# Attention scores of the first token tile ahead of the second tile's last queries

## The chip, the core and the metric

One core of one Trainium2 chip runs the whole program in one launch. The metric is device time in microseconds, median of the runs shown. TensorE (PE) multiplies; its weight loads are listed as PEld. VectorE is DVE, ScalarE is ACT, GpSimd is POOL, and SyncE (SP) issues most transfers.

## What is computed

The reference is an encoder trunk of two layers on 256 tokens of width 1024, in float32: per layer a SwiGLU feed-forward (width 2816), a mixer, and another SwiGLU, each followed by a layer norm of `alpha*x + y`. The mixer of layer 0 is a bidirectional mLSTM; that of layer 1, the stage that is changed, is windowed attention with 16 query heads, 4 key heads, a linear distance bias and a sink logit per head:

```python
p = x @ w_in                                    # queries 1024, keys 256, values 256
s = einsum(q, k) * HEAD_DIM ** -0.5 - slopes * dist
s = where(valid, s, MASK_VALUE)                 # |t - s| <= 128
m = maximum(max(s), sink)
pe = exp(s - m)
attn = pe / (sum(pe) + exp(sink - m))
return einsum(attn, v) @ w_out
```

## The kernel before

**Arithmetic.** Every float32 operand of a large product is split into a high and a low part (`w_hi`, `w_lo`; ACT copies the high part, DVE subtracts for the low one), and `mm3` (line 626) makes three products of it. Tokens lie in two tiles of 128 (`t`), and `xT` holds x transposed. Weights come in words of 128 x 1024; `Weights.split` (line 406) splits a word into a ring of ten buffers.

**Stages.** Six: feed-forward, mLSTM, feed-forward, feed-forward, attention (stage 4, `attn`, line 1223), feed-forward. The end of a stage's second tile (`pending`) is called inside the next stage's first products.

**The attention.** `proj(t, m)` (line 1260) is a projection of 512 columns for token tile t, 24 products into one bank of PSUM: m = 0 makes keys and values, m = 1 the first eight heads' queries, which DVE scales on the way out into `qd`, a tile with the tag `sc`. `k_turn(t)` and `q_turn(t)` (1281, 1287) transpose keys and queries of tile t, four transposes each, into `kk` and `q2`, high part by ACT, low part by DVE. `q_rest` (1295) makes the last eight heads' queries, transposed already, as products of 256 columns; the argument says which part of its 32 pieces, three products each, is made. `scores(j, between)` (1318) makes the scores of step j, heads 2j and 2j+1, for both token tiles: for each tile six products on 64 of the 128 rows (one head in each half of the rows: high x high, high x low, low x high), POOL copies the sink beside them, and DVE adds the bias and takes the row minimum, one instruction a head. Then ACT takes the exponentials, four instructions, with their sums in `sm`. Each score product reads the keys of all 256 tokens, so both `k_turn`s come before it.

Then, step after step (line 1406), `scale` (POOL) divides by the sums, `turn` transposes the weights, `values` multiplies by v and `out_proj` multiplies by the output weights. `fill` puts pieces of `q_rest` and `out_proj` between. The sequence ahead of that loop is

```python
proj(1, 0); k_turn(0); q_turn(0); proj(1, 1)
k_turn(1); q_rest(range(QC[0])); q_turn(1)      # QC[0] is 5
```

**What sets the order.** None of these calls issues anything. `Program` records every operation, and `issue` (line 307) issues them in the order of `ORDER`, a list of steps whose running sums are the numbers of the recorded operations: 6658 of them, for all stages. Each engine works through its own in that order. `SLOTS` says which buffer each tile takes: banks of PSUM (`p`, eight), weights' words, the ring, the attention's `sc` (six), `nm` and `sm` (three).

Of the kernel before, what the change touches and what calls it, by code (L numbers as in the profile page):

```python
# [9 lines left out]
F32 = mybir.dt.float32  # L10
FR = mybir.dt.float32r
AF = mybir.ActivationFunctionType
OP = mybir.AluOpType
# [18 lines left out]
SW = 1  # L32
CT = [0, 1]
# [230 lines left out]
        "503250679835"),  # L264
    "t.0": ("00413152105244534524043241352"),
    "stats": ("000101110010"),
    "mv": ("011101100000"),
    "rs": ("110011110010"),
    "raw.1": ("03101030130120310231230123103210"),
    "wt.1": ("0132"),  # L270
# [1208 lines left out]
```

## Time and profile before

| | us |
|---|---|
| median of 3 runs | 918.23 (917.81 to 919.16) |
| the profiled execution | 918.0 |
| its span, first to last instruction | 916.3 |

The attention's projections begin at about 650 us of the span, its scores run from 670 to 711 us, and the last feed-forward's products are under way at 740 us. The profile's rows give start, duration, engine, operation, and the tile written from the tiles read; nearly all rows carry line 316, the one in `issue` that issues recorded operations, so one goes by tiles: `kk_hir` and `kk_lor` are the keys' parts, `q2r` the queries, `p` a bank of PSUM, `sc` the scores and, under the same tag, keys and queries before they are transposed (products written `p<-ident,sc` are transposes). Records of products overlap, since they are pipelined: what counts is how far apart they start.

### The profile page before, as it was taken

Reading aid. Unit: us, or ns where it says so; the run is one execution under the profiler, and the core shown is the slowest. Engines: PE = TensorE matmul, PEld = TensorE weight load, DVE = VectorE, ACT = ScalarE, POOL = GpSimd, SP = SyncE. Lnnn points to the kernel's source line nnn. Section 1 sums busy time; section 2 is a strip of 40 time slices with the busy share of each in tenths; the row PEclk is TensorE's granted clock in tenths of the full one; section 3 lists DMA queues with packets and bytes.
Section 4 is the critical chain, followed back from the end, with each engine's and each line's share of the span. In section 5 each row is a group of like instructions: output and inputs, shape, how many; then the busy total and the mean of one; then the engine's idle time right before and its main releaser. Section 6 shows DMA issues by size and latency. Waiting matters only on the chain.

```text
span 916.3 us, 12374 instructions
## 1 busy us (share of the span) xinstructions
PE 906.1 (99%) x4397; PEld 750.8 (82%) x4397; DVE 813.9 (89%) x989; ACT 576.9 (63%) x796; POOL 144.2 (16%) x191
## 2 busy tenths in 40 slices
PE   9999999999999999999999999999999999999996
PEld 7888888889988888888888888888887788888885
DVE  7999899987788999889999989899898899987996
ACT  6767567547664577566647674774588657665570
POOL 0211211110101111111011111110345211201110
PEclk9999999999999999999999999999999999999999
DMA  9999798657346899979788998997552287998951
GB/s 336 326 276 293 220 294 209 215 168 259 96 163 241 237 240 230 307 222 277 222 275 207 276 268 249 264 231 247 170 200 70 70 266 204 270 284 236 300 140 46
DMA packets 100654, 208.51 MB, mean 228 GB/s; under 512 B 6864, under 2 KB 21216, under 8 KB 100592
## 3 DMA queue, kind: packets, MB, share of 16 engines
q1 hardware_dynamic: 82816, 173.82, 54.3%
q0 software_dynamic: 17632, 33.64, 22.1%
q8 instruction: 34, 0.56, 0.2%
q10 hardware_dynamic: 144, 0.26, 0.1%
q14 instruction: 28, 0.23, 0.1%
HBM read 206.65 MB, written 1.05 MB: 227 GB/s over the span
## 4 chain that ended last, share of the span: by engine, by line
PE 98%; DVE 1%; DMA 0%; issue 0%; ACT 0%; POOLq 0%; POOL 0%; DVEq 0%
PE p L316 98%; DMA s_raw<-in_at_w_out_dram 0%; DVE x L316 0%; DVE w_lo L316 0%; ACT w_hi L316 0%; POOLq L1475 0%; ACT q2r L316 0%; DVE stats L316 0%; DVE mv L316 0%; POOL ji L316 0%; DVE ident L316 0%; DVE rs L316 0%; POOLq L316 0%; DVEq L316 0%; POOLq L1466 0%
## 5 line engine op out<-in xcount | busy, mean ns | idle before, releaser
L316 ACT CAST w_hi<-s_raw 128x1024 fp32r<-128x1024 f32 x240 | 246.4, 1051 | 94.0 <-PE p L316 51.0
L316 DVE TENSOR_TENSOR w_lo<-s_raw,w_hi 128x1024 fp32r<-128x1024 f32 x240 | 287.3, 1221 | 14.4 <-PE p L316 6.9
L316 DVE TENSOR_TENSOR w_lo<-w_raw,w_hi 128x1024 fp32r<-128x1024 f32 (+1 forms) x166 | 198.5, 1207 | 24.8 <-ACT w_hi L316 19.9
L316 ACT CAST w_hi<-w_raw 128x1024 fp32r<-128x1024 f32 (+1 forms) x166 | 171.0, 1041 | 74.2 <-PE p L316 41.9
L316 PE MATMUL p<-w_hi,xT_hi 128*128 128x512 f32 x512 | 194.6, 395 | 0.0
L316 PE MATMUL p<-w_lo,xT_hi 128*128 128x512 f32 x512 | 194.4, 396 | 0.0
L316 PE MATMUL p<-w_hi,xT_lo 128*128 128x512 f32 x512 | 194.2, 394 | 0.0
L316 PE MATMUL p<-w_lo,h_hir 128*128 128x512 f32 (+1 forms) x323 | 119.8, 390 | 0.0
L316 PE MATMUL p<-w_hi,h_hir 128*128 128x512 f32 (+1 forms) x323 | 119.5, 390 | 0.0
L316 PE MATMUL p<-w_hi,h_lor 128*128 128x512 f32 (+1 forms) x323 | 119.4, 390 | 0.0
L316 PEld LDWEIGHTS p<-w_lo,xT_hi 128*128 128x128 f32 x512 | 96.1, 188 | 19.6 <-DVE w_lo L316 0.3
L316 PEld LDWEIGHTS p<-w_hi,xT_lo 128*128 128x128 f32 x512 | 96.1, 188 | 19.3 <-DVE xT_lo L316 0.3
L316 PEld LDWEIGHTS p<-w_hi,xT_hi 128*128 128x128 f32 x512 | 96.0, 188 | 19.3 <-ACT xT_hi L316 0.6
L316 POOL DMA_DIRECT2D s_raw<-in_ffn_w_in_dram x42 | 50.9, 1220 | 295.8 <-DVE w_lo L316 109.9
L316 PE MATMUL p<-w_hi,S_hir 128*128 128x512 f32 x256 | 96.2, 390 | 0.0
L316 PE MATMUL p<-w_hi,S_lor 128*128 128x512 f32 x256 | 96.1, 389 | 0.0
L316 PE MATMUL p<-w_lo,S_hir 128*128 128x512 f32 x256 | 95.1, 389 | 0.0
L316 PEld LDWEIGHTS p<-w_lo,h_hir 128*128 128x128 f32 x323 | 60.7, 188 | 12.2
L316 PEld LDWEIGHTS p<-w_hi,h_lor 128*128 128x128 f32 x323 | 60.7, 188 | 12.1
L316 PEld LDWEIGHTS p<-w_hi,h_hir 128*128 128x128 f32 x323 | 60.5, 188 | 12.2 <-ACT h_hir L316 0.2
L316 POOL DMA_DIRECT2D w_raw<-in_ffn_w_in_dram x22 | 27.3, 1260 | 192.5 <-DVE s_raw L316 104.3
L316 PEld LDWEIGHTS p<-w_hi,S_hir 128*128 128x128 f32 x256 | 48.1, 188 | 10.9 <-ACT t L316 1.0
(189 smaller groups left out, 1204.3 us busy)
## 6 DMA issues: line engine op xcount, KB each, us to landing
s_raw<-in_ffn_w_in_dram SPq DMA_DIRECT2D x97, 512.0 KB, 6.7
w_raw<-in_ffn_w_in_dram SPq DMA_DIRECT2D x62, 512.0 KB, 6.0
s_raw<-in_ffn_w_out_dram SPq DMA_DIRECT2D x61, 512.0 KB, 5.8
s_raw<-in_ffn_w_in_dram POOLq DMA_DIRECT2D x42, 512.0 KB, 7.3
w_raw<-in_ffn_w_out_dram SPq DMA_DIRECT2D x27, 512.0 KB, 5.4
w_raw<-in_ml_w_in_dram SPq DMA_DIRECT2D x24, 512.0 KB, 4.6
w_raw<-in_ffn_w_in_dram POOLq DMA_DIRECT2D x22, 512.0 KB, 7.2
s_raw<-in_ffn_w_in_dram SPq DMA_DIRECT2D x18, 256.0 KB, 5.1
```

Source lines behind the costliest of these rows:

```text
L316: f(*args, **kw)
```

## The change

`proj` may make a part of its products (`ks`) and hold its bank until the rest; `scores` is taken apart into `half(j, t, banks)`, the six products, POOL's copy and DVE's two instructions for one tile, and `expo(j, t)`, ACT's two; `early(j)` makes both for tile 0 in two banks of its own. With EARLY = 2, steps 0 and 1 have their first tile made early, and their place in the loop makes only the second one, in two more banks. `nm` and `sm` have four buffers.

```diff
-            def proj(t, m):
-                ps = wbank()
-                for k in range(8):
+            def proj(t, m, ks=range(8)):
+                ps = held.pop((t, m)) if ks[0] else wbank()
+                for k in ks:
...
-                if m == 0:
+                if ks[-1] < 7:
+                    held[t, m] = ps
+                elif m == 0:
...
+            def early(j):
+                half(j, 0, [wbank((128, 2, S))[:, 0] for _ in range(2)])
+                expo(j, 0)
+
             def scores(j, between):
...
+                if j < EARLY:
+                    half(j, 1, [wbank((128, 2, S))[:, 0] for _ in range(2)])
                 else:
-                    ps = [wbank((128, 2, S)), wbank((128, 2, S))]
...
+                    ps = [wbank((128, 2, S)) for _ in range(2)]
+                    for t in range(2):
+                        half(j, t, [p[:, t] for p in ps])
                 if between is not None:
                     between()
...
+                for t in range(1 if j < EARLY else 0, 2):
+                    expo(j, t)
...
-            proj(1, 1)
+            proj(1, 1, range(4))
             k_turn(1)
+            early(0)
+            proj(1, 1, range(4, 8))
+            for j in range(1, EARLY - 1):
+                early(j)
             q_rest(range(QC[0]))
+            if EARLY > 1:
+                early(EARLY - 1)
             q_turn(1)
```

`ORDER` and `SLOTS` are replaced whole, for all six stages; the number of operations stays 6658. Read through ORDER, TensorE's queue around the place is, with the number of products of each call (S(j,t) is the score block of step j and tile t):

| | TensorE's queue from the keys' second transposes on |
|---|---|
| before | k_turn(1) 4, proj(1,1) 3, q_rest 1, proj 1, q_rest 1, proj 3, q_rest 8, q_turn(1) 3, S(0,0) 6, q_turn(1) 1, q_rest 11, S(0,1) 6 with one of S(1,0), q_rest 16, S(1,0) 5, q_rest 10, S(1,1) 6 |
| after | k_turn(1) 4, proj(1,1) 1, q_rest 1, proj 12, S(0,0) 6, proj 7, q_rest 10, q_turn(1) 4, q_rest 10, S(1,0) and S(0,1) 12, q_rest 27, S(1,1) 6 |

Ahead of k_turn(1) the old queue has 17 of proj(1,1)'s 24 products and two products of q_rest, the new one 4 and none.

More of the change, by code (lines that the diff above doesn't have):

```diff
@@ L32 @@
 SW = 1
+EARLY = 2
 CT = [0, 1]
@@ L39 @@
 ORDER = (
[207 rows of a table removed]
[206 rows of a table added]
 )
 SLOTS = {
-    "raw.0": ("210375894160ab235798a3b1270586492706351792840a63b5824a0376b12a950371"),
-    "p": ("3275714003260343071152161261516216215555634170524061732573604751024052375104126373674045206243753410"
-        "2763544201141022414410422206137147250124731601566516506116051015601476432475321340245765271430621547"
-        "0166232663126613312621641232570623056410072302032720330732720"),
+    "raw.0": ("321074689152ab307468a3b2140768951804372860951a43b7805a1394b20a671392"),
@@ L253 @@
+    "p": ("7726143024501264721103513501305151053355147653637504627132156370460357046253741062615726304572156721"
+        "5436075712552157251117552517204352641253602217242741271471274744756274530135254730175670532470514605"
+        "16513744024002742207074247001546753460245732060210216062162106164"),
     "h_hir.0": ("01001"),
-    "h_lor.0": ("10101"),
-    "w_hi": ("6768095130964720852931483069218659270964306517289436702158934670215893407659821437580692134758061923"
-        "4785062193478506219837540621973810465279318042736519807562314982365017834296750186293475018629438127"
-        "0654873912605478392106547832051964785320164958370621450938614825793061482579306148290753684219705638"
-        "2479015632074986513207498653027148953046287150439620954268031942356795218036479531028647593820135792"
-        "713098467532"),
@@ L260 @@
-    "w_lo": ("2108424370857191438825409670813427259384713240631879043512685973014268597302749175403682415970821346"
-        "9518026734591082673495018764253941806592834192587316048197236415381087862513209874362150789430524617"
-        "9038274569308172540936807215678943256178024314690173457806213896510478912634805971698430569780416358"
-        "0217945620437986510243798601354276809481396725394082419852763017596803541729506814578192034578021309"
-        "503250679835"),
-    "t.0": ("00413152105244534524043241352"),
@@ L266 @@
[L266 to L270, printed above, removed]
-    "a_hir.1": ("1010"),
-    "a_lor.1": ("1010"),
-    "den.1": ("1101"),
-    "hst.1": ("1111"),
-    "hmv.1": ("0101"),
-    "hrs.1": ("1110"),
-    "h_hir.2": ("0101001010"),
-    "h_lor.2": ("1010110101"),
-    "raw.2": ("8975460317258a96043b86a594703192b47136540891b72a369827ba4035a716ba5803196b425986103b42a716073294a5b9"
-        "32845472a36918b0546198230b5a06743218"),
@@ L281 @@
-    "t.2": ("2301524103213320314352354203204125301153451204025545243544"),
-    "sc.4": ("4212152104531245301452"),
-    "raw.4": ("34203524421301520354"),
-    "nm.4": ("01001202"),
-    "sm.4": ("21212120"),
-    "pr0_hir.4": ("01111110"),
-    "pr0_lor.4": ("00111111"),
-    "pr1_hir.4": ("11101010"),
-    "pr1_lor.4": ("10001011"),
-    "o.4": ("01110101"),
-    "h_hir.5": ("10101"),
-    "h_lor.5": ("01001"),
-    "raw.5": ("102305321b48520639705367a0ab218a90b3871542ab90a68731a9506b059584726b"),
@@ L294 @@
-    "t.5": ("13505412501444130321035034514"),
+    "h_lor.0": ("01010"),
+    "w_hi": ("4874953029716840190254792863407284952713051684937205468193720546819372056413089275106438971205634879"
+        "1208469352174806935248170639452817064589231756804912685097483129865047329157604832915760483901574836"
+        "2091425783601924570863197428610359742681503948076251497306218457930621845793162085491384627503861942"
+        "7053681907425639817024563981720456389170245861937204517396238052317496058271843605927864130527986354"
+        "127834906178"),
@@ new lines @@
+    "w_lo": ("8236425073987610431028793481054310826875931208496351427806981532476091824596471308476529137048269351"
+        "0748690312478569301457826397510462873054218950732456827269241307265103472852910437856214093785042819"
+        "0327628054913267081459365209872314986150472983560791407836952478691325097814920356784193425670278145"
+        "9236071495286731045928763195280476359025417920638059786342701984652793174065928316270618453978269124"
+        "785904265197"),
+    "t.0": ("13015334223502455505412340234"),
@@ new lines @@
+    "stats": ("001011100111"),
+    "mv": ("111001101001"),
+    "rs": ("100010001111"),
+    "raw.1": ("13233213213210122330312103213021"),
+    "wt.1": ("1203"),
+    "a_hir.1": ("1010"),
+    "a_lor.1": ("0101"),
+    "den.1": ("0010"),
+    "hst.1": ("0110"),
+    "hmv.1": ("1110"),
+    "hrs.1": ("0001"),
+    "h_hir.2": ("1010111001"),
+    "h_lor.2": ("0101010101"),
+    "raw.2": ("859764031726859b0a34865b9a7130429a7016ba3842970516482597b01a8536b97a01364b9276a4310b9285341b0269875a"
+        "026794b0825a367195a14632079b0685120b"),
@@ new lines @@
+    "t.2": ("4430251042543542345220120340242312503145315235440352440533"),
+    "sc.4": ("0512432025134021354021"),
+    "raw.4": ("32013214312403150245"),
+    "nm.4": ("01201123"),
+    "sm.4": ("02003013"),
+    "pr0_hir.4": ("01100000"),
+    "pr0_lor.4": ("10011011"),
+    "pr1_hir.4": ("11100001"),
+    "pr1_lor.4": ("10100101"),
+    "o.4": ("01101011"),
+    "h_hir.5": ("01001"),
+    "h_lor.5": ("10101"),
+    "raw.5": ("210332150498b125732b631ba847502a9840a2385067ba4912786a94030bb31594a2"),
@@ L295 @@
+    "t.5": ("35123042540233523553024000125"),
 }
@@ L1258, in attn @@
             pieces = []
-            def proj(t, m):
-                ps = wbank()
-                for k in range(8):
+            held = {}
+            def proj(t, m, ks=range(8)):
+                ps = held.pop((t, m)) if ks[0] else wbank()
+                for k in ks:
                     if t == 0 and m == 1 and k == PEND[bound[0] - 1]:
@@ L1316, in flush @@
                 del lows[:n]
-            def scores(j, between):
-                g = j // 2
-                nm = tile_([128, 2, 2], F32, "nm", bufs=3)
-                sm = tile_([128, 2, 2], F32, "sm", bufs=3)
-                if SW:
-                    p1 = wbank((128, 2, S))
-                    ps = [wbank((128, 2, S)), p1]
-                else:
-                    ps = [wbank((128, 2, S)), wbank((128, 2, S))]
-                for t in range(2):
-                    for n_, (qe, ke) in enumerate(((0, 0), (0, 1), (1, 0))):
-                        for a in range(2):
-                            r = slice(64 * a, 64 * a + 64)
-                            nc.tensor.matmul(ps[a][:, t], q2[r, j, qe, tok(t)], kk[ke][r, g], start=n_ == 0, stop=n_ == 2)
-                    sc[j, t] = tile_([128, 2, 320], F32, "sc", bufs=6)
-                    nc.gpsimd.tensor_copy(sc[j, t][:, :, S], neg_sink[:, 2 * j:2 * j + 2])
-                    for a in range(2):
-                        h = 2 * j + a
-                        nc.vector.tensor_tensor_reduce(sc[j, t][:, a, 0:S], ps[a][:, t], dist[:, t], -slope[h], neg_sink[:, h:h + 1],
-                                                       OP.add, OP.min, accum_out=nm[:, t, a:a + 1])
@@ new lines, in attn, with half @@
+            sums_ = {}
+            def half(j, t, banks):
+                g = j // 2
+                if j not in sums_:
+                    sums_[j] = tile_([128, 2, 2], F32, "nm", bufs=4), tile_([128, 2, 2], F32, "sm", bufs=4)
+                nm, sm = sums_[j]
+                for n_, (qe, ke) in enumerate(((0, 0), (0, 1), (1, 0))):
+                    for a in range(2):
+                        r = slice(64 * a, 64 * a + 64)
+                        nc.tensor.matmul(banks[a], q2[r, j, qe, tok(t)], kk[ke][r, g], start=n_ == 0, stop=n_ == 2)
+                sc[j, t] = tile_([128, 2, 320], F32, "sc", bufs=6)
+                nc.gpsimd.tensor_copy(sc[j, t][:, :, S], neg_sink[:, 2 * j:2 * j + 2])
+                for a in range(2):
+                    h = 2 * j + a
+                    nc.vector.tensor_tensor_reduce(sc[j, t][:, a, 0:S], banks[a], dist[:, t], -slope[h], neg_sink[:, h:h + 1],
+                                                   OP.add, OP.min, accum_out=nm[:, t, a:a + 1])
@@ new lines, in expo @@
+            def expo(j, t):
+                nm, sm = sums_[j]
+                for a in range(2):
+                    nc.scalar.activation(sc[j, t][:, a, 0:S + 1], sc[j, t][:, a, 0:S + 1], AF.Exp, bias=nm[:, t, a:a + 1],
+                                         scale=-1.0, accum_out=sm[:, t, a:a + 1])
+                if t == 1:
+                    stat[j] = sm
+            def early(j):
+                half(j, 0, [wbank((128, 2, S))[:, 0] for _ in range(2)])
+                expo(j, 0)
+            def scores(j, between):
+                if j < EARLY:
+                    half(j, 1, [wbank((128, 2, S))[:, 0] for _ in range(2)])
+                else:
+                    ps = [wbank((128, 2, S)) for _ in range(2)]
+                    for t in range(2):
+                        half(j, t, [p[:, t] for p in ps])
@@ L1338, in scores @@
                 if between is not None:
                     between()
-                for t in range(2):
-                    for a in range(2):
-                        nc.scalar.activation(sc[j, t][:, a, 0:S + 1], sc[j, t][:, a, 0:S + 1], AF.Exp, bias=nm[:, t, a:a + 1],
-                                             scale=-1.0, accum_out=sm[:, t, a:a + 1])
-                stat[j] = sm
+                for t in range(1 if j < EARLY else 0, 2):
+                    expo(j, t)
             def scale(j):
```

413 rows, old and new, of the table ORDER are left out of this document.

## The prediction

> **What bounds the kernel now.** I read the page first, then TensorE's waits, then the stages of the attention by windows, then TensorE's timeline there, product by product. S(j,t) below is the score block of step j (two heads) for token tile t: six products on 64 rows of the array.
>
> ```profile
> span 916.3 us, 12374 instructions
> ...
> PE 906.1 (99%) x4397; PEld 750.8 (82%) x4397; DVE 813.9 (89%) x989; ACT 576.9 (63%) x796; POOL 144.2 (16%) x191
> ...
> PE 98%; DVE 1%; DMA 0%; issue 0%; ACT 0%; POOLq 0%; POOL 0%; DVEq 0%
> ```
> TensorE is busy for 906.1 of 916.3 us and is 98% of the chain that ended last. Its waits are all in two rows:
>
> ```profile
> PE p L316 <- DVE ident L316: 1.5, 1, 1.5
> PE p L316 <- DMA s_raw<-in_at_w_out_dram: 0.3, 1, 0.3
> ```
> The first is the start of the program. The second lies in the attention, and just where the change works. So there is almost no idle time to take away; what else can move is how closely products follow each other, which "busy" hides, since the records of pipelined products overlap. The plain spacing, in the attention's first projections:
>
> ```profile
> 650.25 0.39 PE L316 MATMUL p<-w_hi,xT_hi 128*128 128x512 f32 x1
> 650.48 0.39 PE L316 MATMUL p<-w_hi,xT_lo 128*128 128x512 f32 x1
> 650.71 0.39 PE L316 MATMUL p<-w_lo,xT_hi 128*128 128x512 f32 x1
> ```
> A product of 512 columns lasts 0.39 us and starts 0.23 us after the one before. The windows (columns: busy us and count of PE, PEld, DVE, ACT, POOL, then granted clock, DMA share, GB/s):
>
> ```profile
> 660.00:680.00 20.00, 19.70 (x139) 16.95 (x138) 18.62 (x34) 16.62 (x33) 3.96 (x10) 1.00 0.71 237
> 680.00:700.00 20.00, 20.00 (x133) 15.38 (x131) 17.73 (x48) 16.53 (x48) 10.33 (x24) 1.00 0.14 53
> 700.00:720.00 20.00, 20.00 (x113) 14.63 (x112) 17.91 (x46) 16.47 (x48) 13.35 (x25) 1.00 0.45 148
> ```
> PE is full throughout, DVE nearly: 18.62 of 20 us where the change puts its first scores. DVE is the engine that may be late if its order turns out badly.
>
> **The change part by part.** *Work.* The pieces that are moved are the same: S(0,0) and S(1,0), their four row minima on DVE, four exponentials on ACT, two small copies on POOL. No product, copy or transfer is added or dropped, so TensorE keeps its 4397 products. What changes is the order, and ORDER is replaced whole: all six stages are planned anew. Walking the running sums of both ORDERs through the recorded calls, I find the other stages shuffled only locally, on TensorE by at most 43 places. There the waits table shows nothing to gain; a loss is possible where a weight part comes late.
>
> *Visits.* TensorE goes to the 64-row score blocks and back. What one visit costs, S(1,1):
>
> ```profile
> 676.62 0.28 PE L316 MATMUL p<-xT_hi,w_hi 128*128 128x256 f32 x1
> 676.74 0.28 PE L316 MATMUL p<-xT_lo,w_hi 128*128 128x256 f32 x1
> 676.95 0.39 PE L316 MATMUL p<-kk_hir,q2r 64*128 64x256 f32 x2
> 677.17 0.28 PE L316 MATMUL p<-kk_lor,q2r 64*128 64x256 f32 x2
> 677.29 0.28 PE L316 MATMUL p<-kk_hir,q2r 64*128 64x256 f32 x2
> 677.50 0.51 PE L316 MATMUL p<-xT_hi,w_lo 128*128 128x256 f32 x2
> 677.84 0.28 PE L316 MATMUL p<-xT_hi,w_hi 128*128 128x256 f32 x1
> ```
> Ordinary products of 256 columns start 0.12 us apart (676.62 to 676.74), and score products run two abreast at the same step (677.17 to 677.29). From 676.74 to 677.84 pass 1.10 us, in which three ordinary products (0.36) and three pairs (0.36) would fit in 0.72. A visit costs 1.10 - 0.72 = 0.38 us beside its work. Counted from ORDER, the 16 blocks make 20 visits before: S(0,1) and S(1,0) are cut 7 + 5, S(5,0), S(5,1) and S(6,1) are cut in two, two and three. After, they make 18: S(1,0) and S(0,1) share one visit of twelve products, S(4,0), S(6,0) and S(6,1) are cut in two. Two visits less are 2 x 0.38 = 0.76 us gained, all of it on TensorE and so on the path. Within the visits, products of the same half that follow each other don't pair; counted in steps, 58 before and 54 after, at 0.12 at most 0.48 us more. I take nothing for it, as other transitions (a product behind transposes) shift too, and keep 0.5 us for the range, also on the other side.
>
> The Trainium skill, page "TensorEngine Tiling (Array Packing)", section "Key Properties", says that changing the tiling mode, not just the tile, drains the TensorE; the 0.38 us above agree. By that rule the change as it is called is bad: scores called tile 0 and tile 1 back to back, and now two steps' halves stand apart, two visits more, which would give 918.23 + 0.76 = 919.0. But the queue follows ORDER, not the calls.
>
> *The first visit.* It is dearer than the others:
>
> ```profile
> 669.30 0.55 PE L316 MATMUL p<-ident,sc 128*128 128x128 f32 x3
> 670.15 0.38 PE L316 MATMUL p<-kk_hir,q2r 64*128 64x256 f32 x2 [0.30 <-DMA s_raw<-in_at_w_out_dram]
> 670.34 0.31 PE L316 MATMUL p<-kk_lor,q2r 64*128 64x256 f32 x2
> ...
> 670.69 0.33 PE L316 MATMUL p<-ident,sc 128*128 128x128 f32 x1
> ```
> Three transposes of some 0.1 us would let the scores start at 669.6 or, with the 0.09 of a usual entry (676.95 - 676.74 - 0.12), at 669.7; they start at 670.15, 0.45 us late. The change doesn't take away what the first reader of the keys waits for, it puts that reader earlier. I cost it at no gain, with 0.45 us as the other end, and its worse turn among the rivals.
>
> *Where S(0,0) goes, and what must be ready.* Against the old queue, 7 projection products, 11 of the last queries' and 3 transposes move behind it: 7 x 0.23 + 11 x 0.12 + 3 x 0.1 = 3.2 us earlier. It reads the keys of both tiles. The old path from the keys' transposes:
>
> ```profile
> 666.04 0.60 PE L316 MATMUL p<-ident,sc 128*128 128x128 f32 x4
> ```
> ```profile
> 666.68 0.59 ACT L316 CAST kk_hir<-p 128x512 fp32r<-128x512 f32 x1 [0.60 <-PE p L316]
> ...
> 668.23 1.28 ACT L316 ACT_TABLE_LOAD   x1
> ```
> ```profile
> 663.69 2.36 DVE L316 TENSOR_TENSOR w_lo<-s_raw,w_hi 128x1024 fp32r<-128x1024 f32 x2 [0.19 <-ACT w_hi L316]
> 665.97 1.22 DVE L316 TENSOR_TENSOR w_lo<-w_raw,w_hi 128x1024 fp32r<-128x1024 f32 x1
> 667.10 0.41 DVE L316 TENSOR_TENSOR v0r<-p,v0r 128x256 fp32r<-128x256 f32 x1
> 667.44 0.68 DVE L316 TENSOR_TENSOR kk_lor<-p,kk_hir 128x512 fp32r<-128x512 f32 x1
> 668.55 0.69 DVE L316 TENSOR_TENSOR sc<-p,qs_row 128x512 f32<-128x512 f32 x1 [0.43 <-PE p L316]
> ```
> The low part of the keys is there at 668.12, 2.08 us after the transposes begin. In the new queue these four are followed by 13 projection products and one of the last queries', 0.4 + 13 x 0.23 + 0.12 = 3.5 us, then S(0,0): 1.4 us to spare. DVE has to keep up 3.2 us earlier for that; its new order puts two of the weight parts (1.22 each) behind the keys and v1's low part (0.41, that of v0 above) ahead, 2.0 us of the 3.2. Behind S(0,0) stand the second half of the projection, 7 x 0.23 = 1.6 us, and 10 products of the last queries, 1.2 us, ahead of the queries' transposes, which need the scaling at 668.55's kind (0.69): covered. The table load of 1.28 us stands in the new ORDER far ahead, among stage 3's last copies. It leaves the crowded stretch, but ACT is not on the path: nothing.
>
> The row minima and exponentials, per piece:
>
> ```profile
> L316 DVE CUSTOM_DVE_ANT_0 sc<-p,dist,neg_sink x32: 467/480/485, 670.8 to 711.9; 128x256 f32<-128x256 f32 x32
> L316 ACT ACTIVATE sc<-sc,nm x32: 495/506/522, 672.5 to 713.0; 128x257 f32<-128x257 f32 x32
> ...
> L316 POOL COPY sc<-neg_sink x16: 178/187/519, 666.7 to 710.9; 128x2 f32<-128x2 f32 x16
> ...
> L316 POOL TENSOR_TENSOR dist<-sc,sc x1: 2140/2140/2140, 651.1 to 651.1; 128x512 f32<-128x512 f32 x1
> ```
> Four minima at 0.48 and four exponentials at 0.51 come some 3 us sooner. One of S(0,0)'s two minima stands ahead of the queries' scaling on DVE (0.48 us of delay against 1.2 us of cover), the other behind it and behind one weight part; the exponentials on ACT stand behind the copy of tile 1's queries. The distances are ready at 651.1 + 2.1 = 653.3, long before. Nobody waits for the exponentials sooner than before: the first transposes of weights still come behind the queries' products. So the softmax gains a lead that TensorE, which has fill work, cannot turn into time. SP's transfers only change places among the attention's weights; DMA share is 0.71 there, not full.
>
> *Sum:* -0.76 (visits) + 0 (pairs, first visit, other stages). The profiled execution took 918.0 us, 1.7 outside its span; it becomes 917.2. The median of the runs is 918.23, 0.23 higher: **917.4 us**.
>
> **The rivals.** *No effect:* the saved visits are eaten by small shifts elsewhere. For it: the whole gain is 0.08% of the time, and five stages are replanned. It gives 918.2.
>
> *More:* pairing gains its 0.5 us and the first visit's 0.45 us vanish: -1.7 in all, and a little spacing elsewhere: 916.3. Against it: nothing removes that wait.
>
> *DVE is late with the keys.* If it is 2.4 us late, two weight parts, S(0,0) waits 2.4 - 1.4 = 1.0 us and all of TensorE behind it: net +0.2, 918.5. It decides from 1.4 us on. The same sort of delay elsewhere, one weight part of 1.22 us late in two or three places of the replanned stages, gives 920.0 to 921.0.
>
> *The first scores wait for a transfer* (the other side). The chain of waits leads into S(0,0) thus:
>
> ```profile
> 666.07 4.04 DMA s_raw<-in_at_w_out_dram
> 670.11 0.03 issue
> 670.15 29.99 PE p L316 x212
> ```
> If that wait is real, S(0,0) stood still until a weight of the output projection landed at 670.11, and placed 3.2 us sooner it stands still 3.2 us longer, with TensorE behind it: 918.23 + 3.2 - 0.76 = 920.7. For it: it starts 0.04 us after the landing. Against: it reads keys and queries, no tile of this transfer, and it would decide only if the semaphore waited for is that very transfer's.
>
> **How the numbers follow.** Forecast 0.47; no effect 0.15; more 0.12; DVE late with the keys 0.06; late weight parts in other stages 0.10; the transfer 0.10. A measurement tells about 0.2%, 1.8 us, from no change. Faster by more than that is "more" and the edge of the forecast, 0.14; slower the last two and little else, 0.21; within it 0.65. The range, 916.2 to 920.4, reaches from all gains together to the first late weight parts and leaves out most of the transfer's case.
>
> **What would show it.** Right: TensorE's waits still near 1.8 us, 18 visits of the score rows instead of 20, each 0.4 us beside its work; a dear first visit again, now behind the projection's products; DVE's w_lo row in the middle stages without new waits by PE. Wrong: a wait of over 1 us ahead of the first score row, named DVE kk_lor or DMA s_raw; or PE waits in the feed-forward stages, where the old order had none.

## The result and the profile after

The changed kernel takes 919.9 us (918.78 to 921.67, 20 runs), the kernel before beside it 918.16 (917.64 to 920.1, 20 runs): ratio 1.0016, interval 1.0009 to 1.0022. It is 1.5 us slower by the ratio, 1.7 by the medians. The forecast was 0.8 us faster. The difference lies just within the 0.2% that was called no change, on the other side of it.

The profiled execution took 921.67 us, the longest of its 20, so its waits are rather many. Its page, the same three rows as before:

```profile
span 920.0 us, 12354 instructions
...
PE 907.1 (99%) x4397; PEld 750.3 (82%) x4397; DVE 813.1 (88%) x989; ACT 577.1 (63%) x796; POOL 145.8 (16%) x191
...
PE 85%; DMA 7%; DVE 3%; issue 2%; ACT 1%; POOL 1%; SPq 0%; POOLq 0%; ACTq 0%; DVEq 0%
```

The work is the same: 4397 products, DVE and ACT as busy as before. The chain of waits changed: 98% TensorE became 85%, with DMA at 7%. TensorE's waits (columns: us in total, times, the longest):

```profile
PE p L316 <- DVE ident L316: 1.5, 1, 1.5
PE p L316 <- ACT w_hi L316: 0.8, 1, 0.8
PE p L316 <- DVE t L316: 0.7, 2, 0.5
PE p L316 <- ACT wt L316: 0.4, 1, 0.4
PE p L316 <- POOL sc L316: 0.4, 1, 0.4
PE p L316 <- DVE w_lo L316: 0.3, 1, 0.3
PE p L316 <- ACT t L316: 0.2, 1, 0.2
```

Two rows of 1.8 us in all became seven of 4.3. The DMA row in the attention is gone; of the six new ones only POOL's lies in the attention. `w_hi` and `w_lo` are weights, `t` a feed-forward's activations, `wt` the mLSTM's weights of tokens. Not all of this is the order's: a second profile of the same kernel (e15 below, 918.79 us, the shortest of its 11) has beside the program's start only two rows, `ACT w_hi` with 0.6 us (at 6.75 us) and POOL's 0.4, and 97% TensorE in its chain. The attention's windows:

```profile
660.00:680.00 20.00, 20.00 (x135) 17.22 (x134) 18.16 (x32) 14.75 (x26) 2.65 (x4) 1.00 0.68 241
680.00:700.00 20.00, 19.49 (x137) 15.37 (x135) 17.80 (x47) 17.03 (x49) 12.98 (x28) 1.00 0.35 104
700.00:720.00 20.00, 19.95 (x112) 13.99 (x109) 17.42 (x46) 16.92 (x47) 12.16 (x25) 1.00 0.17 44
```

The 0.30 us that TensorE missed from 660 to 680 us are back, and 0.51 are missing from 680 to 700 instead. The first score visit in TensorE's timeline, where three transposes and a wait stood before:

```profile
669.12 0.39 PE L316 MATMUL p<-w_lo,xT_hi 128*128 128x512 f32 x1
669.44 0.38 PE L316 MATMUL p<-kk_hir,q2r 64*128 64x256 f32 x2
669.66 0.28 PE L316 MATMUL p<-kk_lor,q2r 64*128 64x256 f32 x2
669.78 0.28 PE L316 MATMUL p<-kk_hir,q2r 64*128 64x256 f32 x2
669.98 0.50 PE L316 MATMUL p<-w_hi,xT_lo 128*128 128x512 f32 x1
```

It starts 0.32 us after the product ahead of it, 0.09 more than the usual 0.23: an entry like any other. Nothing was late, neither a transfer nor the keys. In the trace before, eight semaphore instructions stand on TensorE's queue ahead of the first score product, 0.105 us apart from 669.30 to 670.04, where the changed kernel's trace has none. None of the eight stood waiting: each took 0.05 us, and the one for the queue of the transfer that the view named was done at 669.67, before that landing at 670.11. So the 0.45 us were paid for giving out waits, and the landing merely fell next to the start. The distance from the last transpose to the first score product agrees: 0.57 to 0.60 us in the traces with eight of them (before, e3, e4, e11), 0.50 and 0.47 with seven (e2, e6). The Trainium skill, page "Perfetto Trace Analysis", section "Identifying Dependency Chains", says that an instruction that waits on several engines may have semaphore instructions put ahead of it with the further conditions; this trace agrees and prices them.

### The profile page after: what moved, and what is told of

Its sections match the earlier page's. It is cut to its first block, busy times and chain, and to the rows that moved or that the text cites. A ratio compares the mean times of both kernels' runs of the same rounds, so it can differ in the third digit from the quotient of the medians.

```text
span 920.0 us, 12354 instructions
## 1 busy us (share of the span) xinstructions
PE 907.1 (99%) x4397; PEld 750.3 (82%) x4397; DVE 813.1 (88%) x989; ACT 577.1 (63%) x796; POOL 145.8 (16%) x191
## 3 DMA queue, kind: packets, MB, share of 16 engines
HBM read 206.65 MB, written 1.05 MB: 226 GB/s over the span
## 4 chain that ended last, share of the span: by engine, by line
PE 85%; DMA 7%; DVE 3%; issue 2%; ACT 1%; POOL 1%; SPq 0%; POOLq 0%; ACTq 0%; DVEq 0%
PE p L316 85%; DMA s_raw<-in_ffn_w_in_dram 5%; DVE w_lo L316 2%; DMA w_raw<-in_ffn_w_in_dram 1%; DMA w_raw<-in_ml_w_in_dram 1%; ACT w_hi L316 1%; POOL sc L316 0%; DMA x<-in_x_dram 0%; POOL sm L316 0%; ACT wt L316 0%; DVE x L316 0%; DVE t L316 0%; DVE s_raw L316 0%; SPq L316 0%; DVE sc L316 0%
## 5 line engine op out<-in xcount | busy, mean ns | idle before, releaser
L316 DVE TENSOR_TENSOR w_lo<-s_raw,w_hi 128x1024 fp32r<-128x1024 f32 x237 | 283.4, 1219 | 27.6 <-ACT w_hi L316 19.9
L316 ACT CAST w_hi<-s_raw 128x1024 fp32r<-128x1024 f32 x237 | 243.4, 1051 | 86.7 <-PE p L316 52.0
L316 ACT CAST w_hi<-w_raw 128x1024 fp32r<-128x1024 f32 (+1 forms) x169 | 174.1, 1042 | 80.8 <-PE p L316 49.7
L316 DVE TENSOR_TENSOR w_lo<-w_raw,w_hi 128x1024 fp32r<-128x1024 f32 (+1 forms) x169 | 201.9, 1206 | 18.8 <-ACT w_hi L316 10.3
L316 POOL DMA_DIRECT2D s_raw<-in_ffn_w_in_dram x43 | 53.5, 1261 | 298.0 <-DVE w_lo L316 111.9
L316 PE MATMUL p<-w_lo,S_hir 128*128 128x512 f32 x256 | 97.1, 390 | 0.0
```

The lines of the kernel that those rows point to most:

```text
L316: f(*args, **kw)
```

## Experiments

Two theories to begin with. One: the time is lost in the stages that the change doesn't name, whose order and buffers were planned anew, and the attention itself is about even. Two: the attention costs it. ORDER can be taken apart: up to a point in time the operations are issued as one kernel does, behind it as the other does, with buffers renamed at the seam. Two pairs of runs do that. All times stand beside runs of the kernel before on the same chip.

**The attention alone, and all but the attention**

```diff
 # e1: the changed code; whose ORDER and SLOTS
-from 0 us:   changed kernel
+from 0 us:   kernel before
 from 442 us: changed kernel
-from 743 us: changed kernel
+from 743 us: kernel before
 # e2: the code before, the same the other way round (442, 739 us)
```

> The changed code, with the changed kernel's order and buffers from 442 to 743 us alone (the end of stage 3 and the attention), and the order and buffers of the kernel before ahead of it and behind it. If the loss lies in the stages that the change doesn't name (theory one): 917.4 to 918.2 us, the -0.76 of the two visits or a part of it. If the attention itself costs it (theory two): 919.5 to 920.2 us.

918.51 us (before 918.41), ratio 0.9998 (0.9990 to 1.0007): between the two ranges, level with the kernel before.

> The mirror image: the code before, with its own order from 442 to 739 us, so that the attention is as before, and the changed kernel's order and buffers in the other stages. Theory one (the loss lies in the other stages): 919.5 to 920.7 us. Theory two (in the attention): 918.0 to 918.5 us.

920.19 us, ratio 1.0016 (1.0007 to 1.0024): the whole loss, with the old attention. Theory two falls. The attention brings neither loss nor the gain that was forecast.

**One stage at a time**

```diff
 # e3: the code before; ORDER and SLOTS
+up to 143 us: changed kernel
 # e4
+from 744 us: changed kernel
 # e6
+159 to 443 us: changed kernel
 # e9: the changed code
+up to 159 us: kernel before
 # e14: the changed code
+up to 442 us: kernel before
 # e15: the changed kernel as it is
```

> The kernel before, with the changed kernel's order and buffers up to 143 us alone, in the first feed-forward stage. In the one profile of the changed kernel TensorE falls 1.3 us behind by 90 us. Theory one: 918.8 to 919.6 us, the larger part of the loss. Theory two: 918.0 to 918.5 us.

919.26 us, ratio 1.0008 (0.9999 to 1.0016). Part of it is the seam's: this run's profile has a gap of 0.60 us at 144.5 us, where the two orders meet, that neither kernel has.

> The kernel before, with the changed kernel's order and buffers from 744 us alone, in the last feed-forward stage. In the profile of the changed kernel TensorE loses 0.6 us there. Theory one: 918.4 to 918.9 us. Theory two: 918.0 to 918.5 us.

918.54 us, ratio 1.0001 (0.9991 to 1.0011): nothing.

> The kernel before, with the changed kernel's order and buffers from 159 to 443 us alone (the mLSTM stage and most of the third stage). If the losses of the single stages add up, what the first and the last stage left is here: 918.9 to 919.4 us, with waits near 240 and 364 us. Rival (the loss comes from the order as a whole, transfers running late from stage to stage): 918.2 to 918.6 us.

918.84 us (before 918.52), ratio 0.9998 (0.9989 to 1.0007): between the two ranges, so inconclusive. Its profiled execution was its slowest (920.68 us).

> The changed kernel with the order and buffers of the kernel before up to 159 us, the first stage, and its own behind that. If the first stage carries about half of the loss, as the run with it alone says: 918.9 to 919.3 us. If the loss lies in the order as a whole and only adds up over the stages: 919.5 to 920.0 us.

919.77 us (before 918.75), ratio 1.0009 (1.0000 to 1.0018): 0.8 to 1.0 us of the loss are left, within wide bounds. The time lies in the range named for an order that loses as a whole, not in that for a first stage with half of the loss.

> The changed kernel with the order and buffers of the kernel before up to 442 us, the first three stages, and its own behind that. If the loss lies in the first three stages: 1.2 to 1.6 us less than the control, 918.4 to 918.8 us. If it is spread over the order as a whole: at most 0.8 us less than the control.

> The changed kernel as it is, as a control on the same chip: 919.6 to 920.2 us by every theory.

918.55 us and 919.78 us (before 918.17), ratios 1.0005 (0.9995 to 1.0014) and 1.0015 (1.0006 to 1.0023). The first three stages together hold 1.2 us by the medians and 0.9 by the ratios, most of the loss.

Single stages are too small for times that spread by 2 us. The traces tell more, though each shows one execution. I took the starts of TensorE's products number 1, 701, 1401, 2151, 3101, 3701 and 4397 (1.5, 155.9, 276.6, 440.8, 648.2, 755.5 and 907.6 us in the trace before) and list how many us longer each stretch took than there:

| run | first stage | mLSTM | to 441 | to 648 | attention | last |
|---|---|---|---|---|---|---|
| e1 | 1.66 | 0.01 | -0.05 | *0.13* | *-0.01* | -0.05 |
| e14 | 0.35 | -0.01 | -0.03 | *0.11* | *-0.09* | *-0.12* |
| e3 | *1.67* | -0.01 | -0.02 | 0.00 | -0.30 | 0.05 |
| e4 | -0.11 | 0.00 | 0.00 | 0.00 | -0.01 | *0.28* |
| e6 | 1.88 | *1.18* | *0.01* | 0.33 | -0.42 | 0.02 |
| e9 | 0.88 | *0.66* | *0.08* | *0.55* | *0.01* | *-0.11* |
| e2 | *1.29* | *0.44* | *0.02* | 0.37 | -0.25 | *0.10* |
| changed | *1.41* | *0.81* | *0.54* | *0.33* | *-0.06* | *0.69* |
| e15 | *0.35* | *0.43* | *0.01* | *0.11* | *-0.07* | *0.01* |

(In italics where nearly all of a stretch has the changed kernel's order. The 0.33 and 0.37 of e6 and e2 stand behind a seam.) The mLSTM takes its old time, to 0.01 us, in every row with the old order, and 0.43 to 1.18 more in every row with the new: a real loss, taken apart below. The stretch to 648 us loses 0.11 to 0.55 with the new order and nothing with the old one where no seam is ahead of it. The first stage varies by itself: with the old order too it takes up to 1.9 us longer, most of it one wait near 87 us, so these rows don't show what the new order costs there. The old attention also varies, by 0.4 us, and the changed one lies at its slow end (-0.09 to 0.01).

**What the mLSTM's loss is made of.** One part is the same in every trace. Take the stretch from 200.3 to 211.6 us of the trace before, at whose ends both orders have made the same kinds and numbers of products. All nine traces with the new order there, those of e7, e8, e10 and e12 (below) included, take 0.40 us longer, and those with the old order differ by less than 0.01. There is no wait in it. The old order has four transposes on 64 of the 128 rows in one visit:

```profile
208.49 0.39 PE L316 MATMUL p<-w_hi,xT_lo 128*128 128x512 f32 x1
208.81 0.33 PE L316 MATMUL p<-ident,ig 64*128 64x64 f32 x2
208.98 0.29 PE L316 MATMUL p<-ident,fe 64*128 64x64 f32 x2
209.20 0.39 PE L316 MATMUL p<-xT_hi,w_hi 128*128 128x256 f32 x1
209.42 0.28 PE L316 MATMUL p<-xT_lo,w_hi 128*128 128x256 f32 x1
```

The changed kernel has them in two:

```profile
210.78 0.39 PE L316 MATMUL p<-w_lo,xT_hi 128*128 128x512 f32 x1
211.10 0.33 PE L316 MATMUL p<-ident,ig 64*128 64x64 f32 x2
211.36 0.39 PE L316 MATMUL p<-xT_hi,w_lo 128*128 128x256 f32 x1
211.58 0.28 PE L316 MATMUL p<-xT_hi,w_hi 128*128 128x256 f32 x1
...
212.05 0.28 PE L316 MATMUL p<-xT_hi,w_lo 128*128 128x256 f32 x1
212.26 0.33 PE L316 MATMUL p<-ident,fe 64*128 64x64 f32 x2
212.52 0.38 PE L316 MATMUL p<-xT_hi,w_hi 128*128 128x256 f32 x1
212.75 0.28 PE L316 MATMUL p<-xT_lo,w_hi 128*128 128x256 f32 x1
```

From the product ahead to the second one behind, less 0.23 or 0.12 us for each of the two full products in between, the one visit takes 0.58 us and the two take 0.45 and 0.46: 0.33 of the 0.40 us. So the new order has two visits less in the attention and one more here. The other part varies: from 229.1 to 238.1 us, again between equal work, the new order takes 0.01 to 1.05 us longer, and that is the wait that follows.

**What the new waits are.** The mLSTM's, in ACT's and then TensorE's timeline of the changed kernel:

```profile
236.09 1.14 ACT L316 ACTIVATE w_hi<-w_raw,gcol 128x1024 fp32r<-128x1024 f32 x1
237.13 0.35 ACT L316 ACTIVATE wt<-p,ucol 128x128 f32<-128x128 f32 x1
237.38 1.14 ACT L316 ACTIVATE w_hi<-w_raw,gcol 128x1024 fp32r<-128x1024 f32 x1
238.42 2.16 ACT L316 ACTIVATE wt<-p,ucol 128x128 f32<-128x128 f32 x8
```
```profile
239.29 0.40 PE L316 MATMUL p<-w_hi,xT_hi 128*128 128x512 f32 x1
240.12 0.39 PE L316 MATMUL p<-q_hir,k_hir 128*128 128x256 f32 x1 [0.44 <-ACT wt L316]
```

Two weight parts of 1.14 us stand between the copies of scores that free a bank, and the product that needs the bank starts 0.83 us after its neighbour instead of 0.23. The second of these parts is first used by a product at 271.0 us. The kernel before, ACT in the same place:

```profile
235.85 1.16 ACT L316 ACTIVATE wt<-p,ucol 128x128 f32<-128x128 f32 x4
236.85 0.65 ACT L316 ACTIVATE k_hir<-p 128x512 fp32r<-128x512 f32 x1
237.33 0.68 ACT L316 ACTIVATE wt<-p,ucol 128x128 f32<-128x128 f32 x2
```

No weight part stands there. Two more waits of the changed kernel have this shape: at 33.0 us on DVE (an addition of weights ahead of activations that are to be transposed) and at 364.3 us on ACT (a part first used at 370.6 us ahead of a copy that frees a bank). So a third theory: short work that TensorE waits for stands behind weight parts that have time.

```diff
 # e7: the changed kernel, ORDER
-DVE 31 us:  s_raw<-s_raw,w_raw; t<-t,p; t<-t,p
+DVE 31 us:  t<-t,p; t<-t,p; s_raw<-s_raw,w_raw
-ACT 237 us: w_hi<-w_raw,gcol; eight copies wt<-p,ucol
+ACT 237 us: six copies wt<-p,ucol; w_hi<-w_raw,gcol; two copies
-ACT 363 us: w_hi<-w_raw; t<-p; t<-p
+ACT 363 us: t<-p; w_hi<-w_raw; t<-p
 # e8: the same, and e5's move (below)
```

> The changed kernel with three instructions moved, all outside the attention: on VectorE at 31 us an addition of two weight parts goes behind the two activations that the transposes at 33.0 us read; on ScalarE at 237 us a weight part first used at 271 us goes behind the copies of scores that free the bank for the product at 240.1 us; on ScalarE at 363 us a weight part first used at 370.6 us goes behind the copy that frees the bank for the product at 364.3 us. Theory (short work that TensorE waits for stands behind weight parts that have time): the three waits, 0.42, 0.61 and 0.40 us beyond the usual spacing, go; 918.6 to 919.2 us. Rival (TensorE waits in these places because the weights come late as a whole, so that the waits move on): 919.6 to 920.2 us.

> The changed kernel with the three moves and with the transposes of step 1's weights moved as in the other run. Theory: 918.0 to 918.8 us, as fast as the kernel before or a little faster, what is left being transfers that come late. Rival: 919.6 to 920.2 us.

920.79 us and 920.4 us (before 918.52), ratios 1.0022 (1.0013 to 1.0031) and 1.0016 (1.0008 to 1.0025), both above the rival's range too. The theory falls as the cause of the loss. TensorE's waits in e7 (line 307 here is line 316 there, since the list of the order has nine lines fewer):

```profile
PE p L307 <- DVE ident L307: 1.5, 1, 1.5
PE p L307 <- POOL sc L307: 0.4, 1, 0.4
PE p L307 <- ACT w_hi L307: 0.3, 1, 0.3
PE p L307 <- DVE h_lor L307: 0.3, 1, 0.3
PE p L307 <- DVE w_lo L307: 0.2, 1, 0.2
```

The rows `DVE t`, `ACT wt` and `ACT t` are gone, but `DVE h_lor` and `DVE w_lo` stand in their place: gaps of 0.46 us at 37.1 and 0.33 at 366.1 us (`ACT w_hi` is the wait at 6.75 us). Only the wait at 240 us went without heir; the mLSTM lost 0.19 (e7) and 0.31 us (e8) where the table has 0.43 to 1.18. That the move did it is likely and not shown: the stretch around it is back at the old time, to 0.01 us, in both, but with the order as it was it took 0.29 to 1.05 us more in six traces and only 0.04 in e12's. The other two waits moved on to a later reader.

**Transfers or VectorE in the first stage.** The remaining question is what the first stage runs short of. The transfer engines are full there (DMA share 1.06, 0.96 and 1.01 in the windows from 20 to 80 us of the changed kernel), and VectorE is busy 19.2 to 19.5 of each 20 us.

```diff
         for i in order:
+            if i in [421, 433, 504, 513]:   # e10 (changed), e11 (before)
+                continue
             f, args, kw = self.ops[i]
 # e12 (changed): [264, 274, 484, 494]
```

The numbers in brackets are the operations left out: in e10 and e11 four transfers that add a piece of the weights onto another, in e12 four such additions on VectorE.

> The changed kernel without four of the transfers that add a piece of the weights onto another in the first stage (GpSimd's, 512 KB each, issued at 59, 62, 72 and 76 us); the sums lack those pieces. Theory one (TensorE's wait near 87 us comes from weights that land late, the transfer engines being full from 20 to 120 us): no wait there, 918.9 to 919.4 us. Theory two (VectorE, busy 19.4 of each 20 us there, is what has no room): still a wait, 919.6 to 920.1 us.

> The kernel before without the same four transfers. Theory one: the runs in which weights are late near 87 us go, so the median falls a little, 917.8 to 918.2 us, and the runs lie closer together. Theory two: 918.2 to 918.5 us, with the same spread.

> The changed kernel without four additions of weight parts on VectorE in the first stage (at 31, 37, 66 and 72 us, 1.22 us each); the sums lack those pieces, the transfers stay. Theory two (VectorE has no room): the waits at 33 and 87 us go, 918.8 to 919.3 us. Theory one (late transfers): the wait at 33 us may go, the one near 87 us stays in some form, 919.5 to 920.0 us.

e10: 919.93 us, ratio 1.0008 (0.9999 to 1.0017). e11: 918.04 us, ratio 0.9990 (0.9981 to 0.9999), its 11 runs from 917.36 to 918.53 where the 33 of the kernel before go from 917.70 to 921.11. e12: 919.58 us, ratio 1.0003 (0.9994 to 1.0012). In the profiles of e10, e11 and e12 there is no wait near 87 us, but neither is there in e15's, which leaves nothing out, so the traces alone don't settle it. The runs of e11 do for the kernel before: none of the 11 lies above 918.6 us, of the 33 beside them 20 do. So these four transfers bring most of its variation, and it gets faster without them. The changed kernel does not by its median, which lies in theory two's range, and about halfway by its ratio. e12 lands in theory one's range by its median and in theory two's by its ratio. How the first stage's share divides between the two stays open.

**What takes the attention's gain back.** GpSimd's and TensorE's timelines in the changed kernel:

```profile
683.95 1.48 POOL L316 TENSOR_TENSOR sm<-sm,minus_one 128x4 f32<-128x4 f32 x1 [1.13 <-ACT sc L316]
685.53 1.39 POOL L316 TENSOR_SCALAR sc<-sc,sm 128x256 f32<-128x256 f32 x3
686.87 0.19 POOL L316 COPY sc<-neg_sink 128x2 f32<-128x2 f32 x1
687.02 0.48 POOL L316 TENSOR_SCALAR sc<-sc,sm 128x256 f32<-128x256 f32 x1
```
```profile
686.05 0.40 PE L316 MATMUL p<-pr_hir,v1r 128*128 128x512 f32 x1
686.28 0.27 PE L316 MATMUL p<-ident,sc 128*128 128x128 f32 x1
686.98 0.44 PE L316 MATMUL p<-ident,sc 128*128 128x128 f32 x2 [0.42 <-POOL sc L316]
```

Step 1's weights are scaled in four instructions, and one inversion of the sums, four columns (1.48 us), must come first. It needs the sums of both token tiles: that tile 0 was early helps nothing, the inversion waits for tile 1's exponentials. Of the three scalings at 685.53 the second is tile 1's; the transpose that waits reads the third.

```diff
 # e5: e1, ORDER of TensorE
-value product; 3 transposes of step 1; value product; S(3,0); value product
+value product; value product; S(3,0); value product; 3 transposes of step 1
 # e13: e5, and ORDER of GpSimd in steps 1 and 2 (tile, head)
-scale (0,0) (1,0) (0,1) (1,1)      # step 2: (0,0) (1,1) (1,0) (0,1)
+scale (0,0) (0,1) (1,0) (1,1)      # step 2: (0,0) (0,1) (1,1) (1,0)
 # and one output product ahead of S(7,1); e16: the same kernel again
```

> The kernel of the run with the attention alone, with one change: three transposes of step 1's weights, the first of which TensorE runs at 684.9 us and then waits 0.58 us for GpSimd's scaling, stand behind step 0's next two value products and the six score products between them, 1.0 us of work. Theory (the attention gains at its front and gives it back in that new wait): the 0.58 us gap goes, the stretch from the projection's end to the last weights is 0.4 to 0.6 us shorter than in the run with the attention alone, time 917.9 to 918.2 us. Rival (the wait only moves to what the same scaling feeds next): a gap of the same size behind it, and 918.5 us.

918.67 us (before 918.52), ratio 0.9995 (0.9986 to 1.0003). The rival was right: the wait moved to the next step's transposes, at 689.0 us, and grew from 0.58 to 0.84; the attention's stretch takes 107.25 us (107.31 in e1, 107.33 before).

> The run with the transposes later, with two more changes in the attention: GpSimd scales both heads of the first token tile before the second tile in steps 1 and 2, the order in which the transposes read them; and one product of the output projection goes ahead of the last score visit, which waits for its banks. Theory (GpSimd's scaling takes the gain of the visits back): the wait of 0.84 us near 689 us shrinks to under 0.3, the stretch from 650 to 734 us is 0.7 to 1.2 us shorter than in the kernel before, time 917.3 to 918.0 us, faster than both kernels. Rival (the wait moves again): 918.4 to 918.8 us.

> The version with GpSimd's scaling in order a second time, unchanged, for its time alone. If the gain of the visits is real: 917.2 to 917.8 us, 0.6 to 0.8 us under the kernel before. If the first result was chance: within 0.3 us of the kernel before.

e13: 917.4 us (before 918.17), ratio 0.9993 (0.9984 to 1.0002). e16: 917.87 us (before 918.16), ratio 0.9998 (0.9989 to 1.0007). TensorE's waits in e13 are one row, the program's start:

```profile
PE p L307 <- DVE ident L307: 1.5, 1, 1.5
```

The attention's stretch takes 106.64 us in e13 and 106.65 in e16, 0.69 less than in the profile before and 0.27 less than in the shortest trace with the old attention (e6, 107.33 - 0.42): in the traces the gain is there, both times. The times, 0.8 and 0.3 us under the kernel before, don't prove it, since both intervals hold no change, and e16's 917.87 us misses the range named for a real gain and lies, by 0.29 us, within what was called chance. It is the best of the complete versions by its times: the lowest run of each (917.12 and 917.25 us) lies 0.5 under the lowest of the kernel before beside it (917.62 and 917.72).

## Why the prediction was wrong

- *"0 (pairs, first visit, other stages)"*: the 0 for the other stages is the step that failed, and the loss is all there. All but the attention costs the whole 1.5 us (e2), most of it ahead of 443 us (e14 beside e15). The sentence "There the waits table shows nothing to gain; a loss is possible where a weight part comes late" was right in kind, but I gave it 0.10 and the sum nothing. The rival of late weight parts (920.0 to 921.0) came nearest; it is not two or three waits of 1.22 us, though, but waits of 0.2 to 0.8 us, more in one execution than in another, and what is late is a short copy behind a weight part as often as a weight. The steadiest part is no wait at all: the 0.40 us of the mLSTM's second visit to 64 rows. I had counted visits only in the attention; with the one more in the mLSTM, my own price of 0.38 makes the -0.76 a -0.38. The new order doesn't only lose, either: the third stage (278.5 to 444.2 us, between equal work) took 0.25 us less in e6 and e15, and 0.28 more in the first profile, which has the wait at 364 us. The table's cut at 276.6 us hides that, since two transposes and two products have changed sides there.
- *-0.76 for two visits less.* The count was right: 18 visits, S(1,0) and S(0,1) in one of twelve products. The gain wasn't: summed from the rows (entry, inside and exit less 0.12 us a step), 20 visits cost 8.92 us before and 18 cost 8.53 after, 0.39 less, and 0.37 of that is the entry of the first visit (0.46 us, now 0.09). The price of a visit isn't fixed; others became dearer, the last one, S(7,1), most: 0.9 us beside its work where it was 0.55, as it finds its banks unread. GpSimd's new wait of 0.58 takes more than the 0.39, and the net is still -0.06 (107.27 against 107.33); where the other 0.25 us were gained wasn't traced. That GpSimd sets when a step's transposes may start was nowhere in the working; I wrote that nobody waits for the exponentials sooner, and left out that the weights' scaling behind them is a chain of its own.
- *The dear first visit stays: wrong,* and with it "the first scores wait for a transfer". The visit is a usual one now; the wait before was issue, not data.
- *DVE late with the keys:* no such wait in any of these traces, as forecast.
- *What would show it:* the sign named for "wrong", "PE waits in the feed-forward stages", is what came in the first profile, and in the mLSTM too. The mLSTM's second visit stands in no table of waits.
- The range, 916.2 to 920.4, held the time.

Open: what the first stage costs, and which of the moved instructions behind the varying waits costs what. The mLSTM's 0.4 to 1.2 us, with 0.40 of its second visit in them, and the 0.1 to 0.9 of the two stages behind it are shown by traces. Of three waits taken away, two were followed by others, and what the third brought is below what the times can tell.

## What to carry to other kernels

When a change brings a new order of the whole program, the order is the change: price the untouched stages by what each queue has to spare, and where TensorE has no waits left, expect a re-planned stage to lose more than it gains until shown otherwise. What you count in the named stage, such as visits to narrow blocks, count in all of them. Splice the two orders at points where the queues agree, and the share of each stage can be measured if it stands out from the spread; compare traces between points of equal work, and a difference that is the same every time is the order's own, one that varies is a wait's. When a step is split to bring half of it forward, look for the next instruction that needs both halves: it decides.

## What was unexpected about the hardware

- An instruction with many conditions is expensive on TensorE's queue by itself: eight semaphore instructions, 0.105 us each, held the first score product for 0.45 us with everything there, while the view named a transfer.
- A visit to 64-row blocks costs for two small transposes about what it costs for a block of scores (0.38 us in the prediction): with the second one in the mLSTM the stretch took 0.40 us more, in nine traces out of nine, and no view of waits shows it.
- GpSimd's small instructions are long. The changed kernel's rows of the tile `sm` (shortest, median and longest in ns):

```profile
L316 POOL TENSOR_SCALAR sc<-sc,sm x32: 473/478/1450, 679.7 to 719.3; 128x256 f32<-128x256 f32 x32
L316 POOL TENSOR_TENSOR sm<-sm,minus_one x8: 1009/1016/1965, 677.7 to 716.9; 128x4 f32<-128x4 f32 x8
```

  The inversion of 128 x 4 numbers takes 1.02 us, twice a scaling of 128 x 256 (0.48). So a step's scaling is a chain of 1.02 + 4 x 0.48 = 2.9 us, in which the order of the four decides when the transposes can go on.
- Four transfers of the first stage bring most of the kernel's variation: without them the 11 runs of the kernel before spread by 1.2 us, where 33 with them spread by 3.4.
